# When the row loads of an output projection are requested: two tiles ahead, the last heads in pairs, and the next layer's weights behind them

## The chip, the core and the metric

The kernel runs on one core of one Trainium2 chip. The metric is the device time of one execution in microseconds (us), the median of several. Times inside the kernel come from one profiled execution, read through the hardware profiler's trace. Engines are named as the profile names them: PE (TensorE, matrix multiplication), DVE (VectorE), ACT (ScalarE), POOL (GpSimd) and SP (SyncE, which here does nothing but issue DMAs, so that "SPq" is a queue of DMA issues in program order).

## The reference

A two-layer encoder trunk on x of 1024 rows by 1024 columns, float32. Each layer normalises x, projects it by one matrix, runs three kinds of attention on column slices, gates the results and projects the concatenated heads back:

```python
def hybrid_layer(x, ...):
    h = rms_norm(x, g_norm)
    z = jnp.einsum('bsd,dc->bsc', h, w_in)          # 2656 columns
    ...                                             # A: dense GQA, B: windowed GQA with sink, C: latent attention
    o = jnp.concatenate([oa, ob, oc], axis=-1)      # 1024 rows x 1024 columns
    return x + jnp.einsum('bsm,md->bsd', o, w_out)

for l in range(2):
    h = hybrid_layer(h, ...)
return rms_norm(h, final_g)
```

What the change touches is the last line of a layer, `x + o @ w_out`, and what stands next to it in time: at the end of the first layer the norm of the second layer and the first weights of its input projection, at the end of the second layer the final norm.

## The kernel before

Every float32 product is made from three matmuls: each operand is split into a high part and a low remainder, and h·wh, h·wl and lo·wh are summed. The output projection of a layer works through eight **row tiles** `st` of 128 rows. A tile has two column halves `c` of 512; each half sums over eight heads `m`, with three matmuls for each head, so that one (st, c) has 24 matmuls with 512 columns into a PSUM tile `pw_st_c` (in the names below the layer, `pw0_`, is left out, and a number behind the name is the buffer).

The attention stage has left its result, transposed, in the DRAM tensor `d_o`. The rows of a tile come back in two loads: `ol_st_0` holds heads 0 to 5 (128x6x128, 384 KB, two buffers) and `ol_st_6` heads 6 and 7 (128x2x128, 128 KB, one buffer). ACT casts the high part `oh` from it, and DVE replaces the loaded tile by the remainder (`ol<-ol,oh`). The helper `out_rows` requests a load, `out_hl` requests it if that has not been done and then splits it. `x_row` loads the 512 KB of x (tile `y`) to which the product is added.

The tiles 0 and 1 are mostly computed beside the end of attention; `ab_done` writes their loads. The eight tiles then go through the loop `for st in range(NS)`. In it stand, for each tile: the loads and splits of this tile (`x_row`, `out_hl(0, 6, st)`, `out_hl(6, 8, st)`), its matmuls, the addition to `y`, the store of `y`, the norm of the next layer (`xt`, `rs_x`, DVE scaling with `ng`), its transposition on PE (`pt`), whose results go to the tiles `hTh` and `hTl`.

A scheduler orders the instructions of each engine from the program and its own cost model, so that an instruction can stand on its engine well ahead of or behind its place in the text. Two things limit it. A DMA on SP stands behind the one named in `queue_behind[0]` if that is set (helper `dma`). Buffers limit the rest: a load into a tile with two buffers waits until the matmuls that read the tile two before it are done.

In the loop `queue_behind[0]` names the last load of w_out (`wo_ins[0]`). All DMAs that are written after it are free among themselves, among them the `wst` loads, the weights of the next layer's first projection (`stage.load_wv()` at st == 2, `WV_ST = 2`, and those of the projection behind it). A `wst` load is split by POOL (`wh`) and DVE (`wl`).

The loads of the vectors `ng` (the next norm's scale, spread to 128 rows, 512 KB) and, in the last layer, `fg` stand ahead of the loop.

Of the kernel before, what the change touches and what calls it, by code (L numbers as in the profile page):

```python
# [8 lines left out]
F32 = mybir.dt.float32  # L9
F32R = mybir.dt.float32r  # L10
# [35 lines left out]
def kernel(  # L46
# [22 lines left out]
    P = 128  # L69
    S, D = x.shape[1], x.shape[2]  # L70
    DEPTH = norm_g.shape[0]
    NS = S // P
# [155 lines left out]
    for l in range(DEPTH):  # L228
# [453 lines left out]
        with ExitStack() as ph:  # L682
# [113 lines left out]
            class Gqa:  # L796


                def __init__(self, g, qt, m0):
                    self.g, self.qt, self.m0 = g, qt, m0  # L800
                    self.nm = f"{g}{l}_{qt}"
                    self.q, self.loaded = qstack(g, qt, self.nm)
                    self.sm = small.tile([P, 6], F32, tag=f"sm{g}", name=f"sm{self.nm}")
                    self.o = at.tile([P, 3, P], F32, tag="o", name=f"o{self.nm}", bufs=OBUFS)

                def gate(self):
# [73 lines left out]
            if True:  # L880
# [47 lines left out]
                class UnitB:  # L928
# [7 lines left out]
                    def scores(self):  # L936
                        b, kv, nm, k0, k1 = self.b, self.kv, self.nm, self.k0, self.k1
                        n = self.kts * P
                        mo = (k0 - b.qt + 1) * P
                        mx = small.tile([P, 3], F32, tag="bmx", name=f"bmx{nm}")  # L940
                        scs = at.tile([P, 1152], F32, tag="p", name=f"sc{nm}", bufs=PBUFS)
                        scs = [scs[:, g * 384 : (g + 1) * 384] for g in range(3)]
                        for g in range(3):
                            h = 3 * kv + g
                            ps = ps_s(f"s{nm}_{g}")
                            kr_ = slice(k0 * P, k1 * P)
                            mm3(ps[:, :n], [(b.head(h), ks["b", 0][:, kv, kr_]), (b.head(h), ks["b", 1][:, kv, kr_])])
                            sc = scs[g]
                            V.tensor_tensor_reduce(
                                sc[:, :n],  # L950
                                ps[:, :n],
                                mask[:, mo : mo + n],
                                0.125,
                                -3.0e38,
                                ALU.add,
                                ALU.max,
                                mx[:, g : g + 1],
                            )

                        sk = sink[:, 3 * kv : 3 * kv + 3]  # L960
                        nmb = small.tile([P, 3], F32, tag="bnm", name=f"bnm{nm}")
                        V.tensor_tensor(nmb, mx, sk, ALU.max)
                        V.tensor_scalar(nmb, nmb, -1.0, None, ALU.mult)
                        es = small.tile([P, 3], F32, tag="bes", name=f"bes{nm}")
                        V.tensor_add(es, nmb, sk)
                        A.activation(es, es, AF.Exp)
                        for g in range(3):
                            h = 3 * kv + g
                            A.activation(
                                scs[g][:, :n],  # L970
                                scs[g][:, :n],
                                AF.Exp,
                                bias=nmb[:, g : g + 1],
                                accum_out=b.sm[:, h : h + 1],
                            )
                        smv = b.sm[:, 3 * kv : 3 * kv + 3]
                        V.tensor_add(smv, smv, es)
                        self.scs = scs
# [18 lines left out]
            def ab_done():  # L997
                pk_.close()
                vp_.close()
                wa_.oo = wa_.enter_context(tc.tile_pool(name=f"oo{l}", bufs=1, side="right", reuse_waits="tile"))  # L1000
                wa_.wa = wa_.enter_context(tc.tile_pool(name=f"wa{l}", bufs=1, side="right", reuse_waits="tile"))
                for st in range(2):
                    out_rows(0, 6, st)
                for m in range(MW):
                    load_wo(wa_.wa, m)
                    if m == 0:
                        x_row(0)
                for st in range(2):
                    out_hl(0, 6, st)
                x_row(1)  # L1010
                out_hl(6, 8, 0)

            orows, xrows, wo_ins = {}, {}, {}

            def out_rows(m0, m1, st):

                nm = f"{l}_{st}_{m0}"
                orows[m0, st] = h, lo = [
                    wa_.oo.tile([P, m1 - m0, P], F32R, tag=f"o{t}{m0}", name=f"o{t}{nm}", bufs=1 if m0 else 2)
                    for t in "hl"  # L1020
                ]
                dma(lo, d_o[:, m0:m1, st * P : (st + 1) * P])

            def out_hl(m0, m1, st):
                if (m0, st) not in orows:
                    out_rows(m0, m1, st)
                h, lo = orows[m0, st]
                A.copy(h, lo.bitcast(F32))  # L1028
                V.tensor_sub(lo, lo.bitcast(F32), h.bitcast(F32))  # L1029

            def x_row(st):

# [17 lines left out]
            def out_part(st, c, m0, m1):  # L1050

                if m0 == 0:
                    wa_.ps[st, c] = (ps_o if (2 * st + c) % 4 == 3 else ps_s)(f"pw{l}_{st}_{c}")
                cs = slice(c * 512, (c + 1) * 512)
                for m in range(m0, m1):
                    h, lo = (t[:, m % 6, :] for t in orows[m // 6 * 6, st])
                    wh, wl = (t[:, cs] for t in wa_.w[m])
                    mm3(wa_.ps[st, c], [(h, wh), (h, wl), (lo, wh)], m == 0, m == 7)
                    yield
# [150 lines left out]
        with ExitStack() as ph:  # L1210
# [10 lines left out]
            for st in range(NS):  # L1221
                nm = f"{l}_{st}"
                s_ = slice(st * P, (st + 1) * P)
                if st > 1:
                    x_row(st)
                    out_hl(0, 6, st)
                if st:
                    out_hl(6, 8, st)
                y = xrows[st]
                if last:  # L1230
                    ss = small.tile([P, 2], F32, tag="ss2", name=f"ssf{nm}")
                for c in range(2):
                    cs = slice(c * 512, (c + 1) * 512)
                    for _ in out_part(st, c, MW if (st, c) in wa_.ps else 0, 8):
                        pass
                    ps = wa_.ps[st, c]
                    V.tensor_add(y[:, cs], ps, y[:, cs])
                    if last:
                        jk = wb.tile([P, 512], F32, tag="jk", name=f"jkf{nm}_{c}", bufs=2)
                        A.activation(jk, y[:, cs], AF.Square, accum_out=ss[:, c : c + 1])  # L1240
                        if c == 0:
                            e0 = small.tile([P, 1], F32, tag="e0", name=f"e0{nm}")
                            V.tensor_scalar(e0, ss[:, 0:1], 1.0 / D, EPS, ALU.mult, ALU.add)
                            V.tensor_mul(y[:, cs], y[:, cs], fg[:, cs])
                if last:
                    ms = small.tile([P, 1], F32, tag="ms1", name=f"ms_f{nm}")
                    V.scalar_tensor_tensor(ms, ss[:, 1:2], 1.0 / D, e0, ALU.mult, ALU.add)
                    r = small.tile([P, 1], F32, tag="rs1", name=f"rs_f{nm}")
                    G.tensor_tensor(out=r, in0=ms, in1=mhalf[:, 0:1], op=ALU.pow)
                    tc.keep_in_program_order(nc.vector.tensor_mul(y[:, 512:1024], y[:, 512:1024], fg[:, 512:1024]))  # L1250
                    A.activation(y[:, 0:512], y[:, 0:512], AF.Copy, scale=r[:, 0:1])
                    dma(x_dst[s_, 0:512], y[:, 0:512], nc.scalar)
                    V.tensor_scalar(y[:, 512:1024], y[:, 512:1024], r[:, 0:1], None, ALU.mult)
                    dma(x_dst[s_, 512:1024], y[:, 512:1024])
                    continue
                dma(x_dst[s_, :], y)
                if not last:
                    xt = stage.px.tile([P, D], F32, tag="xt", name=f"xt{l + 1}_{st}", bufs=XTB)
                    stage.norm(st, xt, y, xt)
                    if st == WV_ST:  # L1260
                        stage.load_wv()
                    if st < NS - 1:
                        stage.turn(st, xt, ps_t)
                    else:
                        stage.xt = xt


# [70 lines left out]
```

## Time and profile before

| | |
|---|---|
| median of 3 runs | 1338.37 us (1336.61 to 1343.8) |
| profiled execution | 1340.55 us |
| its span, from first to last instruction | 1338.5 us |
| mean granted TensorE clock | 0.991 of full speed |
| PE busy | 1301.4 us, 97% of the span |
| DVE, ACT, POOL busy | 883.6, 720.3, 530.6 us |
| DMA | 166.46 MB, mean 124 GB/s |

A busy share is a mean over stages that have different limits. The rest of the time of the profiled execution, 1340.55 - 1338.5 = 2.05 us, lies outside the span. Tile numbers in the trace are left out, so `ol<-d_o` stands for all row loads; of one size or one time it can be told which it is from the order of instructions. The profile's line numbers are those of the kernel before: L97 is the DMA helper, L136 the three matmuls, L171 the transposition, L1028 and L1029 the two steps of `out_hl`, L1237 the addition to `y`, L219 the `wl` step of a weight tile.

### The profile page before, as it was taken

The numbers are of one execution on the slowest core, as the hardware profiler recorded it, in microseconds if no ns is written. First come the engines' busy times: TensorE is split into PE (matmuls) and PEld (weight loads), VectorE is DVE, ScalarE is ACT, GpSimd is POOL, SyncE is SP. The second block draws the span as 40 slices with busy tenths as digits, with TensorE's granted clock in tenths as the row PEclk, the third lists the DMA queues.
The fourth block names the chain that finished last, engine by engine and source line by source line (L and its number), as shares of the span: only waits on it lengthen the run. The fifth ranks groups of instructions, "written<-read, shape, count | busy, mean of one in ns | idle before, by whom it ended". The sixth has DMA issues, their size and how long they took to land.

```text
span 1338.5 us, 21710 instructions
## 1 busy us (share of the span) xinstructions
PE 1301.4 (97%) x7320; PEld 1136.0 (85%) x7320; DVE 883.6 (66%) x2242; ACT 720.3 (54%) x1551; POOL 530.6 (40%) x602
## 2 busy tenths in 40 slices
PE   7999999999999999998999999999999999999997
PEld 7888998869898898876898889888799988888786
DVE  6685761068888989855437757600888899888543
ACT  5332341168888988732223324311888888886332
POOL 3520121026766676732014201200367766678110
PEclk8999999999999999998999999999999999999999
DMA  7244559264212521346323344791732225114443
GB/s 252 88 136 136 149 197 266 75 162 115 73 55 62 135 54 52 127 142 204 128 89 105 118 135 151 233 226 58 185 94 60 72 65 146 41 36 145 138 153 114
DMA packets 176878, 166.46 MB, mean 124 GB/s; under 512 B 22528, under 2 KB 149376, under 8 KB 176768
## 3 DMA queue, kind: packets, MB, share of 16 engines
q1 hardware_dynamic: 158016, 140.43, 36.7%
q10 hardware_dynamic: 18752, 24.65, 5.3%
q8 instruction: 58, 0.95, 0.3%
q14 instruction: 52, 0.43, 0.1%
HBM read 107.35 MB, written 57.67 MB: 123 GB/s over the span
## 4 chain that ended last, share of the span: by engine, by line
PE 82%; DMA 6%; DVE 4%; ACT 3%; issue 2%; POOL 2%; SPq 1%; POOLq 0%; DVEq 0%; ACTq 0%
PE pg L136 13%; PE pw L136 12%; PE pzb L114 7%; PE pza L114 7%; PE poa L136 6%; PE sc L136 5%; PE ppa L730 5%; PE pzc L136 4%; PE sa L136 4%; PE ppc L730 4%; PE poc L136 3%; PE pob L136 2%; PE pzv L114 2%; PE pzv L136 2%; PE sb L136 2%
## 5 line engine op out<-in xcount | busy, mean ns | idle before, releaser
L711 DVE CUSTOM_DVE_ANT_0 pa<-sa,zero 128x512 f32<-128x512 f32 x96 | 65.4, 681 | 141.0 <-PE sa L136 136.1
L738 POOL TENSOR_SCALAR ptha<-pfa 128x512 fp32r<-128x512 f32 x96 | 59.5, 620 | 208.0 <-ACT pfa L737 207.8
L739 POOL TENSOR_TENSOR ptla<-pfa,ptha 128x512 fp32r<-128x512 f32 x96 | 124.0, 1292 | 5.7
L136 PE MATMUL sa<-ka,qsta 128*128 128x512 f32 x384 | 124.5, 419 | 1.5 <-DVE nmxc L711 0.8
L136 PE MATMUL sc<-k,qc 128*128 128x512 f32 x384 | 113.5, 411 | 3.2 <-DMA qc<-d_qc 3.2
L721 ACT ACTIVATE pa<-pa,nmxa 128x1024 f32<-128x1024 f32 x96 | 111.4, 1161 | 8.8 <-DVE nmxa L711 8.8
L136 PE MATMUL pw<-woh,oh 128*128 128x512 f32 x256 | 102.6, 407 | 12.0 <-ACT oh L1028 10.1
L730 PE MATMUL ppa<-ident,pa 128*128 128x128 f32 x768 | 106.5, 273 | 0.1
L730 PEld LDWEIGHTS ppa<-ident,pa 128*128 128x128 f32 x768 | 91.5, 141 | 15.3 <-DVE ptla L742 0.6
L136 PE MATMUL pw<-wol,oh 128*128 128x512 f32 x256 | 102.6, 402 | 0.1
L136 PE MATMUL pg<-hTh,wh 128*128 128x512 f32 x256 | 100.5, 393 | 0.0
L136 PE MATMUL pg<-hTh,wl 128*128 128x512 f32 x256 | 100.2, 392 | 0.0
L136 PE MATMUL pg<-hTl,wh 128*128 128x512 f32 x256 | 100.2, 391 | 0.0
L136 PE MATMUL pw<-woh,ol 128*128 128x512 f32 x256 | 99.2, 398 | 0.3 <-DVE ol L1029 0.3
L644 ACT ACTIVATE g<-pg 128x512 f32<-128x512 f32 x32 | 19.1, 598 | 137.6 <-PE pg L136 110.2
L136 PE MATMUL poa<-ptha,vAB 128*128 128x384 f32 x256 | 88.1, 344 | 0.6 <-POOL ptla L739 0.3
L218 POOL TENSOR_SCALAR wh<-wst 128x384 fp32r<-128x384 f32 (+1 forms) x52 | 30.1, 596 | 143.8 <-PE pzb L114 79.2
L136 PE MATMUL poa<-ptla,vAB 128*128 128x384 f32 x256 | 86.6, 338 | 0.0
L721 ACT ACTIVATE pc<-pc,nmxc 128x1024 f32<-128x1024 f32 x64 | 74.0, 1156 | 9.8 <-DVE nmxc L711 9.5
L136 PEld LDWEIGHTS sc<-k,qc 128*128 128x128 f32 x384 | 66.3, 189 | 12.3 <-DVE ob L820 2.6
L711 DVE CUSTOM_DVE_ANT_0 pa<-sa,zero,nmxa 128x512 f32<-128x512 f32 x96 | 71.2, 743 | 3.6 <-PE sa L136 0.7
L136 PEld LDWEIGHTS sa<-ka,qsta 128*128 128x128 f32 x384 | 64.5, 189 | 9.7 <-DVE nmxc L711 2.1
(234 smaller groups left out, 3828.2 us busy)
## 6 DMA issues: line engine op xcount, KB each, us to landing
wst<-in_w_in_dram SPq DMA_DIRECT2D x20, 512.0 KB, 3.7
d_gate<-g ACTq DMA_DIRECT2D x32, 256.0 KB, 2.0
wost<-in_w_out_dram SPq DMA_DIRECT2D x32, 256.0 KB, 2.7
wst<-in_w_in_dram SPq DMA_DIRECT2D x16, 384.0 KB, 4.4
qsta<-d_qa SPq DMA_DIRECT2D x64, 96.0 KB, 2.6
qstb<-d_qb SPq DMA_DIRECT2D x64, 96.0 KB, 2.7
k<-d_kn SPq DMA_DIRECT2D x12, 512.0 KB, 6.7
qc<-d_qc SPq DMA_DIRECT2D x96, 64.0 KB, 2.2
```

Source lines behind the costliest of these rows:

```text
L114: return lambda *a, **k: tc.keep_in_program_order(f(*a, **k))
L136: T.matmul(ps, lhsT=a, rhs=b, start=first and i == 0, stop=last and i == len(parts) - 1)
L218: G.tensor_scalar(h, f, 1.0, 0.0, ALU.mult, ALU.add)
L644: A.activation(g, ps, AF.Silu)
L711: V.tensor_tensor_reduce(p[:, c * 512 : (c + 1) * 512], ps, zero[:, 0:1].to_broadcast([P, 512]), -1.0, nmx[0][:, 0:1] if c else 3.0e38, AL ...
L721: A.activation(p, p, AF.Exp, scale=-1.0, bias=nmx[1][:, 0:1], accum_out=sm)
L730: T.transpose(pt[:, (j - q0) * P : (j - q0 + 1) * P], p[:, j * P : (j + 1) * P], ident)
L738: G.tensor_scalar(hi, f, 1.0, 0.0, ALU.mult, ALU.add)
L739: G.tensor_tensor(out=lo, in0=f, in1=hi.bitcast(F32), op=ALU.subtract)
```

## The change

- At the end of tile `st`'s matmuls the rows 0 to 5 of tile st + 2 are requested and split; before, tile st's own were written at its start.
- Heads 6 and 7 are loaded for two row tiles at once (128x2x256, 256 KB, one buffer), four loads in a layer in place of eight. Each tile's part is split by itself. The first pair is written in `ab_done`.
- After these requests `queue_behind[0]` is set to the last row load, so that SP loads written after it, the `wst` loads among them, stand behind it.
- `x_row(st + 2)` moves to the end of tile st.
- Some tiles of a few columns in the attention stage get fewer buffers (`sm` 3, `bmx`, `bnm`, `bes` 2).

```diff
@@ attention, small tiles
-                    self.sm = small.tile([P, 6], F32, tag=f"sm{g}", name=f"sm{self.nm}")
+                    self.sm = small.tile([P, 6], F32, tag=f"sm{g}", name=f"sm{self.nm}", bufs=3)
...
@@ ab_done
                 x_row(1)
+                out_rows(6, 8, 0, 2)
                 out_hl(6, 8, 0)
...
+            def out_rows(m0, m1, st, n=1):
+                lo = wa_.oo.tile(
+                    [P, m1 - m0, n * P], F32R, tag=f"ol{m0}", name=f"ol{l}_{st}_{m0}", bufs=1 if m0 else 2
+                )
+                wo_ins["o"] = dma(lo, d_o[:, m0:m1, st * P : (st + n) * P])
+                for i in range(n):
+                    orows[m0, st + i] = lo[:, :, i * P : (i + 1) * P]
 
             def out_hl(m0, m1, st):
-                if (m0, st) not in orows:
-                    out_rows(m0, m1, st)
-                h, lo = orows[m0, st]
+                lo = orows[m0, st]
+                h = wa_.oo.tile([P, m1 - m0, P], F32R, tag=f"oh{m0}", name=f"oh{l}_{st}_{m0}", bufs=1 if m0 else 2)
                 A.copy(h, lo.bitcast(F32))
                 V.tensor_sub(lo, lo.bitcast(F32), h.bitcast(F32))
+                for m in range(m0, m1):
+                    orows[m, st] = h[:, m - m0, :], lo[:, m - m0, :]
...
@@ the loop over row tiles
-                if st > 1:
-                    x_row(st)
-                    out_hl(0, 6, st)
-                if st:
-                    out_hl(6, 8, st)
                 y = xrows[st]
...
+                if st < NS - 2:
+                    out_rows(0, 6, st + 2)
+                    out_hl(0, 6, st + 2)
+                    if st % 2:
+                        out_rows(6, 8, st + 1, 2)
+                    queue_behind[0] = wo_ins["o"]
+                if st < NS - 1:
+                    out_hl(6, 8, st + 1)
...
                     else:
                         stage.xt = xt
+                    if st < NS - 2:
+                        x_row(st + 2)
```

How the scheduled programs differ, at the end of the first layer. First SP's queue there, from the norm's scale `ng` on. Before:

```order
L97 DMA ng_7365<-in_norm_g_dram 128x1024
L97 DMA ol_2_0_7494<-d_o_86 128x6x128
L97 DMA ol_1_6_7444<-d_o_86 128x2x128
L97 DMA x_69<-y_0_6818 128x1024
L97 DMA d_o_86<-oc_1_6_7052 128x256
L97 DMA y_2_7491<-in_x_dram 128x1024
L97 DMA wst_1_7564<-in_w_in_dram 128x4x128 x2
L97 DMA wst_2_7573<-in_w_in_dram 128x4x128 x2
L97 DMA wst_3_8284<-in_w_in_dram 128x2x512
L97 DMA wst_4_8292<-in_w_in_dram 128x2x512
L97 DMA ol_3_0_7599<-d_o_86 128x6x128
L97 DMA ol_2_6_7499<-d_o_86 128x2x128
```

The same place of SP's queue with the change:

```order
L97 DMA ng_7365<-in_norm_g_dram 128x1024
L97 DMA ol_2_0_7420<-d_o_86 128x6x128
L97 DMA x_69<-y_0_6816 128x1024
L97 DMA d_o_86<-oc_1_6_7052 128x256
L97 DMA y_2_7451<-in_x_dram 128x1024
L97 DMA ol_3_0_7473<-d_o_86 128x6x128
L97 DMA ol_2_6_7478<-d_o_86 128x2x256
L97 DMA x_69<-y_1_6864 128x1024
L97 DMA ol_4_0_7560<-d_o_86 128x6x128
L97 DMA y_3_7506<-in_x_dram 128x1024
L97 DMA wst_1_7577<-in_w_in_dram 128x4x128 x2
L97 DMA wst_2_7586<-in_w_in_dram 128x4x128 x2
```

Six `wst` loads, `wst_1` to `wst_4`, stood ahead of `ol_3_0`; now none does, and the first comes behind `ol_4_0` and `y_3`. `wst_3` and `wst_4` have moved further back, behind `ol_7_0` and the last pair, `wst_5` and `wst_6` behind `y_7`. `ol_2_0` keeps its place right behind `ng`; `ol_1_6` is gone from here, as it is part of the first pair.

Next PE, the last part of row tile 1, behind the transposition of tile 0 (`pt_0`). Before:

```order
L171 MATMUL pt_0_1_7436<-ident,xt_0_7421 128x128 x4
L136 MATMUL pw_1_0_7318<-woh_7_7389,oh_1_6_7443 128x512
L136 MATMUL pw_1_0_7318<-wol_7_7390,oh_1_6_7443 128x512
L136 MATMUL pw_1_0_7318<-woh_7_7389,ol_1_6_7444 128x512
L136 MATMUL pw_1_1_7334<-woh_5_7369,oh_1_0_6805 128x512
L136 MATMUL pw_1_1_7334<-wol_5_7370,oh_1_0_6805 128x512
L136 MATMUL pw_1_1_7334<-woh_5_7369,ol_1_0_6806 128x512
```

With the change:

```order
L171 MATMUL pt_0_1_7437<-ident,xt_0_7429 128x128 x4
L136 MATMUL pw_1_1_7334<-woh_5_7369,oh_1_0_6861 128x512
L136 MATMUL pw_1_1_7334<-wol_5_7370,oh_1_0_6861 128x512
L136 MATMUL pw_1_1_7334<-woh_5_7369,ol_1_0_6804 128x512
L136 MATMUL pw_1_1_7334<-woh_6_7379,oh_1_6_7425 128x512
L136 MATMUL pw_1_1_7334<-wol_6_7380,oh_1_6_7425 128x512
L136 MATMUL pw_1_1_7334<-woh_6_7379,ol_0_6_6866 128x512
```

The last reader of `ol_1_0`, whose buffer `ol_3_0` takes, has moved four rows forward, from row 2711 of PE's order to row 2707, and the last reader of the first pair (`ol_0_6`) stands on row 2713. The first matmul of tile 3 (`pw_3_0` with `oh_3_0`) stands on row 2731 in both programs, with `oh_2_6` four rows behind it; the transposition of tile 1, `pt_1`, moves from row 2761 to row 2739.

Last DVE, behind the scaling of `xt_1` at which tile 1 ends, with the change:

```order
L164 SCALAR_TENSOR_TENSOR xt_1_7484<-y_1_6864,rs_x_1_7489,ng_7365 128x1024
L1030 TENSOR_TENSOR ol_3_0_7473<-ol_3_0_7473,oh_3_0_7475 128x768
L1030 TENSOR_TENSOR ol_2_6_7478<-ol_2_6_7478,oh_2_6_7480 128x2x128
L178 TENSOR_TENSOR hTl_0_7359<-pt_1_0_7492,hTh_0_7358 128x4x128
L1030 TENSOR_TENSOR ol_4_0_7560<-ol_4_0_7560,oh_4_0_7562 128x768
L178 TENSOR_TENSOR hTl_0_7359<-pt_1_1_7499,hTh_0_7358 128x4x128
L1235 TENSOR_TENSOR y_2_7451<-pw_2_0_7508,y_2_7451 128x512
L219 TENSOR_TENSOR wl_1_7579<-wst_1_7577,wh_1_7578 128x512 x2
L1235 TENSOR_TENSOR y_2_7451<-pw_2_1_7534,y_2_7451 128x512
L1030 TENSOR_TENSOR ol_2_6_7478<-ol_2_6_7478,oh_3_6_7565 128x2x128
L219 TENSOR_TENSOR wl_2_7588<-wst_2_7586,wh_2_7587 128x512 x2
```

Before, the four steps of `wl_1` and `wl_2` stood together right behind the scaling of `xt_0`, ahead of tile 0's `hTl`, and four more (`wl_3`, `wl_4`) around the last addition to `y_1`. Now two stand between the additions to `y_2`, two behind the remainder of `oh_3_6`, and the four others behind the remainders of the last pair.

## Rows read from the trace of the kernel before

**Rows 1.** The page: busy time of each engine, share, instructions.

```profile
PE 1301.4 (97%) x7320; PEld 1136.0 (85%) x7320; DVE 883.6 (66%) x2242; ACT 720.3 (54%) x1551; POOL 530.6 (40%) x602
```

**Rows 2.** Busy time in stretches: length, engines' busy us, PEclk, DMA share, GB/s.

```profile
590.00:600.00 10.00, 7.50 (x32) 5.86 (x31) 3.84 (x6) 2.54 (x5) 2.34 (x2) 0.83 0.24 85
...
630.00:730.00 100.00, 100.00 (x561) 87.19 (x560) 47.72 (x91) 26.73 (x53) 18.20 (x23) 1.00 0.35 110
```

**Rows 3.** PE's waits from 580 to 700: us in total, times, longest.

```profile
PE pw L136 <- ACT oh L1028: 7.8, 2, 5.6
PE pw L136 <- DVE ol L1029: 0.3, 1, 0.3
```

**Rows 4.** The chain that ended last, 585 to 640: start, us, what.

```profile
586.17 6.85 DMA ol<-d_o
593.04 0.84 ACT oh L1028
...
607.82 2.77 DVE wl L219 x3
...
611.06 5.83 DMA ol<-d_o
...
616.97 0.84 ACT oh L1028
...
617.86 9.27 PE pw L136 x30
```

**Rows 5.** The DMA queue of SP in order of time, 585 to 611.

```profile
585.70 0.42 SPq L97 DMA_DIRECT2D ng<-in_norm_g_dram  x1
586.17 4.02 SPq L97 DMA_DIRECT2D ol<-d_o  x2
...
600.29 0.33 SPq L97 DMA_DIRECT2D y<-in_x_dram  x1
600.72 10.24 SPq L97 DMA_DIRECT2D wst<-in_w_in_dram  x6
```

**Rows 6.** Matmuls of `pw` alone, in stretches: PE busy, PEld, DVE, PEclk, DMA.

```profile
611.87:617.86 5.99, 0.40 (x3) 0.01 (x1) 0.68 (x1) 0.82 1.00 280
617.86:622.65 4.79, 4.79 (x11) 3.79 (x12) 0.00 (x0) 0.51 1.04 324
1257.25:1262.00 4.75, 4.75 (x13) 3.43 (x14) 0.68 (x1) 0.64 0.00 0
```

**Rows 7.** The chain that ended last, second layer's projection.

```profile
1249.78 6.56 DMA ol<-d_o
...
1274.27 44.55 PE pw L136 x195
```

**Rows 8.** DMA issues at 632, 611, 628, 585.7 and 600.7: KB, median us to landing.

```profile
ol<-d_o SPq DMA_DIRECT2D x1, 384.0 KB, 3.2
...
ol<-d_o SPq DMA_DIRECT2D x1, 384.0 KB, 5.8
...
ol<-d_o SPq DMA_DIRECT2D x1, 128.0 KB, 2.2
...
ng<-in_norm_g_dram SPq DMA_DIRECT2D x1, 512.0 KB, 6.0
...
wst<-in_w_in_dram SPq DMA_DIRECT2D x4, 256.0 KB, 5.0
```

**Rows 9.** ACT and DVE in order of time, 595 to 599.

```profile
595.50 1.06 ACT L162 ACTIVATE xt<-y 128x1024 f32<-128x1024 f32 x1 [1.62 <-DVE y L1237]
...
597.88 1.28 DVE L164 SCALAR_TENSOR_TENSOR xt<-y,rs_x,ng 128x1024 f32<-128x1024 f32 x1
```

**Rows 10.** ACT at 1226, POOL at 705, in order of time.

```profile
1226.53 0.40 ACT L1028 CAST oh<-ol 128x256 fp32r<-128x256 f32 x1 [2.13 <-DMA ol<-d_o]
...
705.62 1.20 POOL L218 TENSOR_SCALAR wh<-wst 128x512 fp32r<-128x512 f32 x2 [10.62 <-PE pzv L136]
```

More of the change, by code (lines that the diff above doesn't have):

```diff
@@ L939, in scores @@
                         mo = (k0 - b.qt + 1) * P
-                        mx = small.tile([P, 3], F32, tag="bmx", name=f"bmx{nm}")
+                        mx = small.tile([P, 3], F32, tag="bmx", name=f"bmx{nm}", bufs=2)
                         scs = at.tile([P, 1152], F32, tag="p", name=f"sc{nm}", bufs=PBUFS)
@@ L960, in scores @@
                         sk = sink[:, 3 * kv : 3 * kv + 3]
-                        nmb = small.tile([P, 3], F32, tag="bnm", name=f"bnm{nm}")
+                        nmb = small.tile([P, 3], F32, tag="bnm", name=f"bnm{nm}", bufs=2)
                         V.tensor_tensor(nmb, mx, sk, ALU.max)
                         V.tensor_scalar(nmb, nmb, -1.0, None, ALU.mult)
-                        es = small.tile([P, 3], F32, tag="bes", name=f"bes{nm}")
+                        es = small.tile([P, 3], F32, tag="bes", name=f"bes{nm}", bufs=2)
                         V.tensor_add(es, nmb, sk)
@@ L1010, in ab_done @@
                 x_row(1)
+                out_rows(6, 8, 0, 2)
                 out_hl(6, 8, 0)
             orows, xrows, wo_ins = {}, {}, {}
[L1015 to L1022, printed above, removed]
+            def out_rows(m0, m1, st, n=1):
[5 more added lines that the diff above has]
+                    orows[m0, st + i] = lo[:, :, i * P : (i + 1) * P]
             def out_hl(m0, m1, st):
-                if (m0, st) not in orows:
-                    out_rows(m0, m1, st)
-                h, lo = orows[m0, st]
+                lo = orows[m0, st]
+                h = wa_.oo.tile([P, m1 - m0, P], F32R, tag=f"oh{m0}", name=f"oh{l}_{st}_{m0}", bufs=1 if m0 else 2)
                 A.copy(h, lo.bitcast(F32))
                 V.tensor_sub(lo, lo.bitcast(F32), h.bitcast(F32))
+                for m in range(m0, m1):
+                    orows[m, st] = h[:, m - m0, :], lo[:, m - m0, :]
             def x_row(st):
@@ L1055, in out_part @@
                 for m in range(m0, m1):
-                    h, lo = (t[:, m % 6, :] for t in orows[m // 6 * 6, st])
+                    h, lo = orows[m, st]
                     wh, wl = (t[:, cs] for t in wa_.w[m])
@@ L1265 @@
                         stage.xt = xt
+                    if st < NS - 2:
+                        x_row(st + 2)
 _INS = [
```

## The prediction

> **What bounds the kernel now.** I read the page first. PE is busy for 97% of the span [rows 1], so a change pays only where PE stands still or runs below its clock. The busy time in stretches around the output projections shows where that is: between 590 and 600 PE is busy for 7.50 of 10 us, while the 100 us from 630 on are full at a clock of 1.00 [rows 2]. Third, PE's own waits between 580 and 700: only the projection waits, 7.8 us in two pieces for the cast `oh`, the longer one 5.6, and 0.3 for a remainder `ol` [rows 3]. Fourth, the chain that ended last says what is behind the cast [rows 4]. The first piece is `ol_2_0`: its load is issued at 586.17, takes 6.85, is cast by 593.88, and PE goes on at 593.9. The second is `ol_3_0`: issued at 611.06, landed 5.83 later, cast at 616.97, first matmul at 617.86. Ahead of that issue the chain runs through the weight conversions `wl`. SP's queue shows why: behind `y` at 600.29 stand six `wst` issues that take 10.24 us together, because they wait for staging buffers which POOL and DVE free [rows 5]. The row load was ready to go long before; it stood behind weights that nobody needs yet.
>
> The stall costs more than its idle time. The last matmul before it starts at 611.87, 5.99 us before the next [rows 6], where the usual step is 44.55/195 = 0.228 us [rows 7]. So 5.99 - 0.23 = **5.76 us** are idle. The eleven matmuls behind it take 4.79 us at a granted clock of 0.51 [rows 6], which is the lower of the two levels, 1.2 GHz in place of 2.4. At the usual step they take 11 x 0.228 = 2.51, so **2.28 us** more are lost after PE has stood idle. In layer 2 there is one stall, of the first kind: `ol_2_0` issued at 1249.78, 6.56 to landing [rows 7], and from 1257.25 on thirteen matmuls in 4.75 where 2.96 would do [rows 6].
>
> **The change, part by part.** *The weights behind the row loads.* With the change nothing stands on SP between `y_2` (600.29) and `ol_3_0`, so the load goes when its buffer is free. Its buffer is that of `ol_1_0`, whose last reader now stands on PE's row 2707; 23 matmuls lie between its end and row 2731, the first use of `oh_3_0`. That use would come at 611.87 + 0.23 = 612.10 without a wait, so the buffer is free at 612.10 - 23 x 0.228 = 606.9. The load then has the DMA engines nearly to itself. Landing took 3.2 us for this size alone and 5.8 behind weights [rows 8]; I take 3.2, since the weights are now behind it: 610.1. ACT does `xt_1` first: row 2713 ends at 612.10 - 17 x 0.228 = 608.2, the addition to `y` takes at most the 2.77/3 = 0.92 of a `wl` step over as many columns [rows 4], so 609.1, and `xt` 1.06 and a little for its sum [rows 9]: 610.3. The cast takes 0.84 [rows 4]: 611.2, **0.9 us before PE asks**. With 5.8 it is 613.6 and PE waits 1.5.
>
> The pair with heads 6 and 7 is issued when row 2713 is done, 608.2. Its 256 KB lie between 128 KB in 2.2 and 384 KB in 3.2 [rows 8]; midway is 2.7, so 610.9, or 611.4 at 3.2. Cast behind the other one, 0.40 [rows 10], it is ready by 611.8; PE needs it four matmuls after 612.10, at 613.0. `pt_1`, which has moved forward to 613.9 (four matmuls later), needs `xt_1` scaled by DVE: for `xt_0` that was done 597.88 + 1.28 - 595.50 = 3.7 us after ACT's start on it [rows 9], hence 609.1 + 3.7 = 612.8. So the stall goes wholly, with slacks near 1 us: **-5.76 - 2.28 = -8.04**.
>
> *Two heads of tile 1 ahead on PE.* At 593.9 PE now does four matmuls that need only casts before the first remainder, which covers the wait of 0.3 [rows 3]: -0.2.
>
> *The first stalls.* `ol_2_0` keeps its place behind `ng`, in layer 2 behind `fg`. `ng` takes 6.0 us to land and `ol_2_0`, issued 0.47 later [rows 5], takes 6.85 [rows 4], against 3.2 alone [rows 8]. I leave both stalls as they are: 0. The Trainium skill, "DMA: Bandwidth & Descriptors", section "Queues, rings and completion order", has a rule for it: a transfer's completion write on a DMA engine lands only after every earlier write of that engine. By that rule `ol_2_0` cannot be complete before `ng`; the trace agrees (585.70 + 6.0 = 591.7 for `ng`, 593.0 for `ol_2_0`).
>
> *The weights, later.* `wst_1` and `wst_2` are issued behind `ol_4_0` (612.1) and `y_3`, from about 613.1 to 614.3, and land 5.0 later [rows 8], at 619.3; with 8 for the queue ahead of them 622. DVE now converts `wl_1` between the additions to `y_2` and `wl_2` right behind the remainder of `oh_3_6`, which PE needs on row 2788: 613.9 + 0.87 for `pt_1` + 47 x 0.228 = 625.5. From 619.3, POOL's 1.2 [rows 10], two `wl` at 0.92 each, an addition and the remainder make 623.1. Cover is 2.4 us; without it PE waits what is over and loses about 2.3 in clock. Later still: `wst_3` and `wst_4` stand ahead of `y_6`'s addition with some 4 us of room by the order, and the last ones are not urgent, since POOL's `wh` at 705.62 waits 10.62 us for PE, not for data [rows 10]. So 0, at worst +0.5.
>
> *The pairs.* Eight loads become four a layer: four DMA issues fewer on SP, which costs PE nothing either way. The first pair doubles a load at whose end ACT waits: in layer 2 for 2.13 us [rows 10]. 128 KB more at the 280 GB/s of rows 6 are 0.5 us at most; ACT's next exponential moves by that, PE by less. I take +0.1, with bounds 0 and +0.5. The smaller buffers of the attention stage leave all orders there as they were: 0. In layer 2 no weights stand ahead of `ol_3_0`, and its buffer is free four matmuls earlier, while its cast now stands behind a square for the final norm: 0, bounds -0.2 and +0.5.
>
> **The sum.** -8.0 - 0.2 + 0.1 = -8.1 us. The profiled execution would go from 1340.55 to 1332.4. It lies 2.2 above the median of the runs, 1338.37; from the median the same difference gives 1330.3, which I give as **1330.5 us** (-0.6%).
>
> **The rivals.** *The wait comes back in part.* `ol_3_0` lands in 5.8 as before, as `x<-y`, `y` and the pair share the engines: 1.5 of idle plus up to 2.3 at the low clock, so 3.8 of the 8.1 return: 1334.3. For it speaks that 3.2 was seen with the queue quiet; against it, that nothing large is in flight at 606.9.
>
> *No gain.* Another wait on the same path, say `xt_1` or the remainder of `ol_3_0` behind `pt_1` on DVE, stops PE for 5 to 6 us, and the low clock follows again: about 1338. Against it the slacks of 1 us and more, each from a row.
>
> *Slower: the single pair buffer.* A pair can be requested only when the last matmul on the pair before it is done, and PE needs the new one 22 matmuls (5.0 us) later at tile 2, and 28 matmuls and a transposition (7.2 us) later at tiles 4 and 6. Issue, landing, cast and remainder are 0.4 + landing + 0.4 + 0.4, so it decides at a landing above 3.8 and 6.0. At the 6.85 seen behind `ng` the waits are 3.0 and 0.9 us, each with about 2.2 at the low clock: 2 x 5.2 + 4 x 3.1 = 22.8 over both layers, less 8.1: 1353. For it: weights are in flight before tile 4 of layer 1; against it: only 1 MB of them, issued over 10 us before that pair, and none in layer 2. The rule of the Trainium skill named above bears on this too, as a pair's completion would come after that of weights issued ahead of it; no row of the kernel before shows a pair behind weights.
>
> *Better.* Without `ol_1_6` beside it `ol_2_0` lands as if alone, and both first stalls go, about 4 us each with their slow matmuls: 1322. Against it `ng`, which is still ahead; half of that, 1326, is the nearest I would give weight to.
>
> **Chances.** The stall goes and nothing returns: 0.68. In part 0.15, no gain 0.08, slower 0.05, better 0.04. The range reaches from the better half-case to past the partial return: 1327.0 to 1336.5; what lies outside is most of the last three. A difference of 0.5% is 6.7 us, about what a measurement of this kernel can tell from no change, and that line is at 1331.7, so close to the forecast that a fifth of the main case falls short of it. Faster: 0.68 x 0.8 + 0.04 = 0.58; slower 0.05; within 0.5% the rest, 0.37.
>
> **What would show it.** In the changed profile PE's waits between 580 and 700 hold one wait of 2.2 for `oh` and none of 5.6; the stretch from 600 to 630 is full at clock 1.00; `ol_3_0` is issued near 606.9 and lands within 3.5; `wst` issues start after 612. A first stall at 593.9 that is shorter, a wait of PE for `oh` at tiles 4 or 6, or an `ol` landing above 6 there would make it wrong, as would a new wait for `wl` through `y_2`.

## The result, and the profile after

The changed kernel takes 1328.21 us (median of 6 runs, 1326.7 to 1331.22), the kernel before in its runs beside it 1337.76: the ratio is 0.9928, interval [0.9911, 0.9946]. The difference of 9.5 us, 7.2 to 11.9 by the interval, is a little more than the 8.1 forecast. The profiled execution took 1331.22 us with a span of 1329.4, against 1340.55 and 1338.5.

PE's waits of the changed kernel from 580 to 700, which answer to [rows 3]:

```profile
PE pw L136 <- ACT oh L1029: 2.0, 1, 2.0
```

The wait of 5.6 us and that for a remainder are gone; one of 2.0 is left. The chain that ended last, in the same stretch as [rows 4] (start, us, what):

```profile
586.34 6.58 DMA ol<-d_o
592.92 0.02 issue
592.94 0.84 ACT oh L1029
593.78 0.04 issue
593.83 11.00 PE pw L136 x40
604.82 0.87 PE pt L171 x8
605.70 7.76 PE pw L136 x34
613.46 0.87 PE pt L171 x8
614.33 13.89 PE pw L136 x61
```

The first half reads as before: `ol_2_0` behind the vector, 6.6 us. From 593.83 on the chain holds nothing but PE, where before it went through `wl`, a DMA and a cast. Busy time in stretches (length, PE, PEld, DVE, ACT, POOL, PEclk, DMA share, GB/s):

```profile
590.00:600.00 10.00, 7.97 (x36) 6.46 (x35) 4.26 (x6) 2.55 (x5) 1.30 (x2) 0.83 0.29 102
600.00:610.00 10.00, 10.00 (x50) 8.34 (x49) 2.83 (x5) 2.41 (x5) 0.03 (x1) 1.00 0.38 103
610.00:620.00 10.00, 10.00 (x50) 8.33 (x49) 5.44 (x7) 3.37 (x6) 0.79 (x2) 1.00 0.84 264
```

From 610 to 620 fifty matmuls run at a clock of 1.00; before, PE was idle for over half of this and the clock behind it was 0.51 [rows 6]. SP's queue, in order of time, shows why:

```profile
599.28 0.33 SPq L97 DMA_DIRECT2D y<-in_x_dram  x1
606.43 1.75 SPq L97 DMA_DIRECT2D ol<-d_o  x2
608.54 0.33 SPq L97 DMA_DIRECT2D x<-y  x1
611.67 0.36 SPq L97 DMA_DIRECT2D ol<-d_o  x1
612.61 0.34 SPq L97 DMA_DIRECT2D y<-in_x_dram  x1
613.00 2.42 SPq L97 DMA_DIRECT2D wst<-in_w_in_dram  x4
```

`ol_3_0` is issued at 606.43, forecast 606.9, in place of 611.06, and the weights follow at 613.0, forecast 613.1. The DMA issues from 606 to 608 (KB, us to landing), then ACT and PE in order of time:

```profile
ol<-d_o SPq DMA_DIRECT2D x1, 384.0 KB, 3.3
ol<-d_o SPq DMA_DIRECT2D x1, 256.0 KB, 3.4
```

```profile
609.81 0.83 ACT L1029 CAST oh<-ol 128x768 fp32r<-128x768 f32 x1
611.32 0.41 ACT L1029 CAST oh<-ol 128x256 fp32r<-128x256 f32 x1 [0.67 <-DMA ol<-d_o]
```

```profile
611.93 0.39 PE L136 MATMUL pw<-woh,oh 128*128 128x512 f32 x1
...
612.84 0.39 PE L136 MATMUL pw<-woh,oh 128*128 128x512 f32 x1
```

The row load lands in 3.3 us (I took 3.2), its cast ends at 610.64, 1.3 us ahead of PE's first use at 611.93. The pair takes 3.4, not the 2.7 I took, and its cast ends at 611.73, 1.1 us ahead of PE's use at 612.84.

How long each projection takes can be read from one kind of its matmuls (ns min/median/max, first and last start). Before, first and second layer:

```profile
L136 PE MATMUL pw<-woh,oh x128: 387/389/796, 563.8 to 682.2; 128*128 128x512 f32 x128
L136 PE MATMUL pw<-woh,oh x128: 387/389/658, 1226.8 to 1330.9; 128*128 128x512 f32 x128
```

With the change:

```profile
L136 PE MATMUL pw<-woh,oh x128: 387/389/628, 563.9 to 673.5; 128*128 128x512 f32 x128
L136 PE MATMUL pw<-woh,oh x128: 387/389/628, 1218.1 to 1321.8; 128*128 128x512 f32 x128
```

The first layer's projection goes from 118.4 to 109.6 us, the second's from 104.1 to 103.7. These 8.8 and 0.4 us are the whole 9.1 by which the span is shorter, to rounding: nothing was gained elsewhere.

### The profile page after: what moved, and what is told of

Same layout as the page of the kernel before. It is cut to its first block, busy times and chain, and to the rows that moved or that the text cites. A ratio compares the mean times of both kernels' runs of the same rounds, so it can differ in the third digit from the quotient of the medians.

```text
span 1329.4 us, 21686 instructions
## 1 busy us (share of the span) xinstructions
PE 1298.0 (98%) x7320; PEld 1134.1 (85%) x7320; DVE 883.2 (66%) x2242; ACT 720.8 (54%) x1551; POOL 530.3 (40%) x602
## 4 chain that ended last, share of the span: by engine, by line
PE 83%; DMA 5%; POOL 3%; ACT 3%; DVE 2%; issue 2%; SPq 1%; POOLq 0%; ACTq 0%; DVEq 0%
PE pg L136 13%; PE pw L136 11%; PE poa L136 7%; PE pzb L114 7%; PE pza L114 7%; PE ppa L730 5%; PE pzc L136 5%; PE sa L136 5%; PE sc L136 4%; PE ppc L730 3%; PE poc L136 3%; PE pob L136 2%; PE sb L136 2%; PE pzv L114 2%; PE pzv L136 2%
## 5 line engine op out<-in xcount | busy, mean ns | idle before, releaser
L730 PE MATMUL ppc<-ident,pc 128*128 128x128 f32 x512 | 71.9, 273 | 0.8 <-ACT rbb L792 0.7
```

The lines of the kernel that those rows point to most:

```text
L730: T.transpose(pt[:, (j - q0) * P : (j - q0 + 1) * P], p[:, j * P : (j + 1) * P], ident)
```

## The experiments

All times are medians in us. The kernel before was run beside the kernels of each of three groups (e1 to e4, e5 to e8, e9 to e11); between groups the ratios are to be compared.

| run | kernel | time | before | ratio, interval |
|---|---|---|---|---|
| e1 | changed, weights free on the queue | 1338.02 | 1338.28 | 1.0001 [0.9988, 1.0013] |
| e2 | before, weights behind row loads | 1326.48 | 1338.28 | 0.9916 [0.9903, 0.993] |
| e3 | changed, no pairs | 1330.08 | 1338.28 | 0.9942 [0.993, 0.9955] |
| e4 | changed, vector behind `ol_2_0` | 1323.85 | 1338.28 | 0.9897 [0.9883, 0.9912] |
| e5 | changed, again | 1329.2 | 1339.81 | 0.9915 [0.9902, 0.9927] |
| e6 | as e3, again | 1332.67 | 1339.81 | 0.9944 [0.9931, 0.9956] |
| e7 | changed, no early requests | 1334.62 | 1339.81 | 0.9955 [0.9943, 0.9966] |
| e8 | changed, vector loaded by ACT | 1324.56 | 1339.81 | 0.9883 [0.987, 0.9896] |
| e9 | as e4, again | 1323.31 | 1340.15 | 0.9886 [0.9869, 0.9903] |
| e10 | as e4, no pairs | 1325.25 | 1340.15 | 0.9896 [0.9879, 0.9914] |
| e11 | changed, 512 KB more ahead of `ol_2_0` | 1334.27 | 1340.15 | 0.9961 [0.9948, 0.9975] |

### e1: the weights free again

```diff
-                    queue_behind[0] = wo_ins["o"]
```

> The changed kernel without its last line on the queue: the weight loads are again free to stand ahead of the row loads, and by the program's order they do (wst_1 to wst_4 ahead of ol_3_0, as before); early requests and pairs stay. Theory (the place of ol_3_0 behind the weights on SP is the whole stall): PE waits 5 to 6 us for oh near 612 again, the landing of ol_3_0 is 5 us or more, and the time goes back to 0.998 to 1.001 of the kernel before, 1336 to 1339 us. Rival (the early request and the pairs bring the gain, the queue does not matter): 0.992 to 0.994, 1327 to 1330 us, no wait near 612.

The whole gain is gone. SP's queue and PE's first matmul of tile 3 in this kernel, in order of time:

```profile
599.72 10.06 SPq L97 DMA_DIRECT2D wst<-in_w_in_dram  x6
609.88 1.00 SPq L97 DMA_DIRECT2D ol<-d_o  x2
...
616.09 0.79 PE L136 MATMUL pw<-woh,oh 128*128 128x512 f32 x1 [6.00 <-ACT oh L1029]
616.68 0.63 PE L136 MATMUL pw<-wol,oh 128*128 128x512 f32 x1
617.11 0.63 PE L136 MATMUL pw<-woh,oh 128*128 128x512 f32 x1
```

These are the rows of before: six weight issues of 10 us, the row load behind them, a wait of 6.0, and matmuls that start 0.43 apart in place of 0.23. Early requests and pairs alone bring nothing that can be told from zero (the interval reaches 1.7 us to either side), since the program order of a request does not set its place on the queue. The theory holds, the rival falls.

### e2: the order alone

```diff
@@ the kernel before
-                dma(lo, d_o[:, m0:m1, st * P : (st + 1) * P])
+                wo_ins["o"] = dma(lo, d_o[:, m0:m1, st * P : (st + 1) * P])
...
                 if st:
                     out_hl(6, 8, st)
+                    queue_behind[0] = wo_ins["o"]
```

> The kernel before with one thing alone: DMAs written after a tile's row loads stand behind them on SP. Requests stay at their own tile, heads 6 and 7 are loaded tile by tile. By the program's order only wst_1 and wst_2 (1 MB) still stand ahead of ol_3_0, wst_3 to wst_6 have gone behind the last row loads. Theory: ol_3_0 is issued when its buffer is free, near 607, but lands behind 1 MB of weights in 5 to 6 us, so PE waits 0.5 to 2.5 us near 612 and then runs slow for about 2 us: 1331 to 1334 us, ratio 0.995 to 0.998. Rival (the order alone is enough): 1328 to 1330 us, no wait. Rival (only the early request helps): 1336 us or more, wait of 5 us.

It is faster than I expected, and as fast as the changed kernel as far as the intervals tell (ratio 0.9916 against 0.9928, and 0.9915 in e5): one line of order, without early requests and pairs, brings as much. The first rival was right as to the wait near 612. PE's waits from 580 to 700, then ACT in order of time:

```profile
PE pw L136 <- ACT oh L1028: 0.9, 1, 0.9
```

```profile
594.32 0.40 ACT L1028 CAST oh<-ol 128x256 fp32r<-128x256 f32 x1 [0.46 <-DMA ol<-d_o]
594.63 0.36 ACT L763 COPY ohc<-poc 64x256 f32<-64x256 f32 x1
596.63 0.84 ACT L1028 CAST oh<-ol 128x768 fp32r<-128x768 f32 x1 [1.64 <-DMA ol<-d_o]
```

`ol_3_0` is issued at 606.68 and lands behind 1 MB of weights in 5.5, as expected, but PE does not wait for it. By the program's order the scheduler has also put the rest of row tile 1 ahead of tile 2 on PE, so that tile 1's buffers come free sooner and tile 3 is asked for 14 rows later (twelve matmuls and the transposition of tile 1). For the same reason the first wait is not for `ol_2_0`, whose cast ends at 597.5 without a wait of PE, but 0.9 us for the small load of heads 6 and 7. The edit is one line, but it is not one effect: the order of PE changed with it.

### e3, e6 and e10: without the pairs

```diff
@@ ab_done
-                out_rows(6, 8, 0, 2)
+                out_rows(6, 8, 0)
@@ the loop
-                    if st % 2:
-                        out_rows(6, 8, st + 1, 2)
-                    queue_behind[0] = wo_ins["o"]
                 if st < NS - 1:
+                    out_rows(6, 8, st + 1)
+                    queue_behind[0] = wo_ins["o"]
                     out_hl(6, 8, st + 1)
```

> The changed kernel with heads 6 and 7 loaded tile by tile as before (eight loads of 128 KB a layer); early requests and order stay. Theory (pairs cost and bring nearly nothing): 1328 to 1330 us, ratio 0.993 to 0.995, PE's only waits in the projections those at the first use of oh of tile 2, with 0.3 us for a remainder in layer 1 of the trunk since PE's order ahead of it is again that of before. Rival (the pairs bring the part of the gain beyond 8.1): 1 us or more slower than the changed kernel. Rival (the pairs cost, by the load at the end of which ACT waits): faster than the changed kernel by 0.5 us or more.

The kernel is 1.9 us slower than the changed one was in its own runs, but the two intervals overlap. So I ran both beside each other (e5, e6):

> The changed kernel itself once more, as the measure for the runs beside it on the same chip. By both theories 1326.5 to 1331 us, ratio 0.992 to 0.994; if runs differ by the low clock behind the first waits, a run with a granted clock of 0.993 is 2 to 4 us longer than one of 0.997.

> The changed kernel with heads 6 and 7 loaded tile by tile, now beside the changed kernel. In e3 it was 1330.1 against 1328.2 us measured apart. Theory (pairs bring little): within 1 us of the changed kernel beside it. Rival (pairs bring what exceeds the 8.1 forecast): 1.5 to 2.5 us slower than it.

Now the difference is 3.5 us, and the intervals of the two ratios do not touch: the kernel with pairs is the faster one, where I had the pairs at +0.1. PE's waits of e6 from 580 to 700:

```profile
PE pw L136 <- ACT oh L1029: 1.7, 1, 1.7
PE pw L136 <- DVE ol L1030: 0.3, 1, 0.3
```

The 0.3 us for a remainder, which the pairs had covered by two casts that stand ready, are back, but the wait ahead of it is 0.3 us shorter: both kernels wait 2.0 us in this projection. The waits do not explain the difference. e10 is to take the first wait away as well (the edit of e4 added to the above):

> The kernel of e4 with heads 6 and 7 loaded tile by tile. With pairs the changed kernel was 1.9 and 3.5 us faster than without (e3, e6). Theory (the pairs act only through the first wait: two casts of two tiles stand ready for PE before the first remainder, so that the 0.3 us wait and part of the slow matmuls go): with the first wait gone the pairs are worth nothing, within 1 us of e9. Rival (the pairs save on the DMA queue throughout): 2 us or more slower than e9.

It is 1.9 us slower than e9 beside it, but the intervals overlap widely, so this does not decide between the two. Nor is the first wait quite gone in the first layer, as the theory asks, where e9 has no wait for `oh` or `ol`:

```profile
PE pw L136 <- ACT oh L1029: 0.3, 1, 0.3
PE pw L136 <- DVE ol L1030: 0.3, 1, 0.3
```

### e4 and e9: the vector behind the first row load

```diff
             if last:
                 fg = wb.tile([P, D], F32, name="fg", bufs=1)
-                dma(fg, final_g.partition_broadcast(P))
-            else:
-                dma(stage.ng, norm_g[l + 1].partition_broadcast(P))
+            out_rows(0, 6, 2)
+            queue_behind[0] = wo_ins["o"]
+            if last:
+                dma(fg, final_g.partition_broadcast(P))
+            else:
+                dma(stage.ng, norm_g[l + 1].partition_broadcast(P))
...
-                    out_rows(0, 6, st + 2)
+                    if st:
+                        out_rows(0, 6, st + 2)
```

> The changed kernel with the 512 KB loads of ng and fg moved on SP's queue from right ahead of ol_2_0 to right behind it. Theory (ol_2_0 lands late because the vector's load is ahead of it): ol_2_0 lands in 3.3 to 4.5 us in place of 6.3 to 6.6, both first waits of PE (2.0 us each) and the slow matmuls behind them (1.7 us each) go: 7.5 us off the changed kernel, 1320 to 1322 us, ratio 0.987. Rival (the two loads share the DMA engines whichever is first): landing 5.5 us or more, half of the wait stays, 1325 to 1328 us. Rival (what the vector feeds becomes late: the scaling of xt_0 or of y_0): no gain, and DVE waits for ng.

PE's order is the same as in the changed kernel, row for row. Neither projection has a wait for `oh` any more. The DMA issues from 585.5 to 588 (KB, us to landing):

```profile
ng<-in_norm_g_dram SPq DMA_DIRECT2D x1, 512.0 KB, 5.6
ol<-d_o SPq DMA_DIRECT2D x1, 384.0 KB, 4.9
```

`ol_2_0` takes 4.9 us in place of 6.6: late enough to tell that the vector behind it still takes part of the DMA engines, early enough for PE. The gain is 4.4 us on the median, less than the 7.5 expected. The 7.5 counted on the low clock behind both first waits, as in the first profile of the changed kernel: e4's profiled execution (1323.56) is 7.7 us shorter than that one (1331.22), but 3.2 shorter than e5's (1326.75), which has the low clock behind neither. Again:

> The kernel of e4 once more (vectors behind ol_2_0, pairs), as the measure for e10 and e11 beside it. 1322.5 to 1325.5 us, ratio 0.988 to 0.991, no wait of PE for oh in either projection.

1323.31 us, with an interval that ends at 0.9903 (0.9912 in e4), where those of the changed kernel begin at 0.9911 and, in e5, 0.9902. This version beats the kernel before by far more than the uncertainty, and the changed kernel by 4 to 6 us, at the edge of what the intervals separate.

### e8: the vector loaded during attention

```diff
-                dma(fg, final_g.partition_broadcast(P))
+                dma(fg, final_g.partition_broadcast(P), nc.scalar)
...
-                dma(stage.ng, norm_g[l + 1].partition_broadcast(P))
+                dma(stage.ng, norm_g[l + 1].partition_broadcast(P), nc.scalar)
```

> The changed kernel with the loads of ng and fg issued by ACT during attention, long before ol_2_0. Theory (ol_2_0 is late by what is ahead of it on the DMA engines): it lands in 3.2 to 3.5 us, the first waits of PE are gone, 1322 to 1325 us as in e4. Rival (the wait belongs to the late issue of ol_2_0, behind the store of attention's result on SP, not to the vector): the landing is as short but a wait of 0.5 us or more stays, 1326 us or more. Against both: ACT's own work is delayed by the issue, under 0.5 us a layer.

The DMA issue of `ol_2_0` at 589.6 (KB, us to landing):

```profile
ol<-d_o SPq DMA_DIRECT2D x1, 384.0 KB, 3.4
```

With nothing of the vector beside it the load lands in 3.4, and PE has no wait for `oh` in either projection, though the load is issued 3.3 us later than in the changed kernel. But PE's order has changed here too: six matmuls of tile 1 now stand ahead of tile 2. PE begins them at 592.97 and `oh_2_0` at 594.34, and the cast ends at 593.92, so that by the changed kernel's order a wait of about 1.0 us would be left (an estimate from these rows). The absence of a wait in e8 therefore does not refute the rival that blames the late issue; e4 does, where PE's order is unchanged, the load is issued no earlier (586.71 against 586.34) and the wait is gone. Nor is the time of this run the landing's alone.

### e11: more ahead of the first row load

```diff
+            more = dram.tile([P, D], F32, name=f"more{l}")
+            dma(more, x_src[0:P, :])
             for st in range(NS):
```

> The changed kernel with one more transfer of 512 KB (a copy of 128 rows of x within DRAM, whose result nothing reads) ahead of ol_2_0 in each layer, behind the vector. Theory (what stands ahead of ol_2_0 sets its landing, and PE pays its wait and the slow matmuls behind it): landing 1.5 to 4 us longer, 8 to 10.5, the two waits of PE 3.5 to 6 us each, slow matmuls worth 1.7 to 2.3 us behind each in every run: 1332 to 1340 us, ratio 0.995 to 1.001. Rival (the landing is set by ol_2_0 itself or its late issue): unchanged, 1327 to 1330 us.

SP's queue in order of time, the DMA issues from 588 to 592 (KB, us to landing), and PE's waits from 580 to 700:

```profile
588.94 0.42 SPq L97 DMA_DIRECT2D ng<-in_norm_g_dram  x1
589.41 0.56 SPq L97 DMA_DIRECT2D more<-in_x_dram  x1
590.01 0.58 SPq L97 DMA_DIRECT2D ol<-d_o  x1
```

```profile
ng<-in_norm_g_dram SPq DMA_DIRECT2D x1, 512.0 KB, 6.2
more<-in_x_dram SPq DMA_DIRECT2D x1, 512.0 KB, 6.9
ol<-d_o SPq DMA_DIRECT2D x1, 384.0 KB, 7.6
```

```profile
PE pw L136 <- ACT oh L1029: 3.6, 1, 3.6
```

The landing goes up by 1.0 us, less than the 1.5 to 4 of the theory, and the wait by 1.6, as the load is also issued 0.6 us further behind `ng` (1.07 against 0.47). In the second layer the landing is 6.6 and the wait 3.3, where the changed kernel has 6.3 and 2.0, and in e5 5.4 and 1.1. The time rises by 4 to 6 us by ratio (0.9961 against the changed kernel's 0.9928 and, in e5, 0.9915). In the first layer the landing goes from 3.4 with nothing over 4.9 with the vector behind and 6.6 with the vector ahead to 7.6 with a further 512 KB: it follows what shares the engines, and most what stands ahead. The last step is the least certain, as one program's landing can differ by 0.9 us between two executions (6.3 and 5.4 above), and a few rows of PE's order have moved in e11.

### e7: without the early requests

```diff
@@ the loop: requests at the start of their own tile
+                if st > 1:
+                    x_row(st)
+                    out_rows(0, 6, st)
+                    out_hl(0, 6, st)
+                    if st % 2 == 0:
+                        out_rows(6, 8, st, 2)
+                if st:
+                    out_hl(6, 8, st)
+                    queue_behind[0] = wo_ins["o"]
                 y = xrows[st]
...
-                if st < NS - 2:
-                    out_rows(0, 6, st + 2)
-                    out_hl(0, 6, st + 2)
-                    if st % 2:
-                        out_rows(6, 8, st + 1, 2)
-                    queue_behind[0] = wo_ins["o"]
-                if st < NS - 1:
-                    out_hl(6, 8, st + 1)
...
-                    if st < NS - 2:
-                        x_row(st + 2)
```

> The changed kernel without the early requests: row loads are written at the start of their own tile as before, pairs and the order behind the row loads stay. wst_1 and wst_2 stand ahead of ol_3_0 again, and PE asks for oh_3_0 14 rows and a transposition later than in the changed kernel and for oh_4_0 right after. Theory from e2 (the order on the queue brings the gain, the early request nothing): no wait above 1 us behind 600, 1326 to 1330 us. Rival (the early request keeps the loads of tiles 3 and 4 off PE's path): a wait of 1 to 3 us for oh near 612 to 618 and slow matmuls behind it, 1331 us or more.

The rival was right. PE in order of time, and the DMA issues from 610 to 613:

```profile
617.35 0.58 PE L136 MATMUL pw<-woh,oh 128*128 128x512 f32 x1 [3.33 <-ACT oh L1029]
```

```profile
ol<-d_o SPq DMA_DIRECT2D x2, 384.0 KB, 6.0
```

`ol_3_0` and `ol_4_0` are issued behind 1 MB of weights and take 6.0 us each; PE waits 3.3 us. Beside e5 the kernel is 5.4 us slower, though still 5.2 faster than the kernel before. So in the kernel with pairs the early request is not idle: the weights are held only behind requests that are written before them, and with requests two tiles ahead `ol_3_0` and `ol_4_0` are among these. In e2 the same `wst` loads stood ahead of `ol_3_0`, but the queue ran 4 us earlier there: `ol_2_6`, which is ahead of the weights and waits for a buffer of tile 1, was issued at 602.79 in e2 and at 606.59 in e7, and `ol_3_0` at 606.68 and 610.67. With single loads and its own order on PE, e2 needs no early request.

## Why the prediction was right, and where a size was off

**The stall at tile 3.** Right in place, cause and size. Forecast were 5.76 us of idle and 2.28 of slow matmuls; PE's wait of 5.6 has gone and the stretch behind it runs at 1.00. e1 shows the cause: with the weights free on the queue the wait is 6.0 again and the time is that of before; and in e2 the order alone, with the other order on PE that comes with it, takes the wait away. The steps on the way (606.9, 3.2, 611.2, 613.1, 623.1) came out as 606.43, 3.3, 610.64, 613.00 and 623.44, the last one being the end of the remainder of `oh_3_6` on DVE, to be read off this row with its neighbour `wl_2` behind it:

```profile
623.03 0.41 DVE L1030 TENSOR_TENSOR ol<-ol,oh 128x256 fp32r<-128x256 f32 x1
623.36 1.28 DVE L219 TENSOR_TENSOR wl<-wst,wh 128x512 fp32r<-128x512 f32 x2
```

Two of these steps hide errors that did no harm. The terms named for 623.1 come to as much as 623.7, if the addition takes the 0.92 allowed for one elsewhere and the remainder 0.4. And the four weight loads landed in 6.2 us (median), not 5.0.

**The wait for a remainder.** In the first layer it is gone, as forecast. In the second one of 0.3 us has come in its place, which I had not seen.

**The first stalls.** Forecast 0; in the first profile each is 0.2 us shorter (2.02 and 1.98 against 2.23 and 2.24). The prediction named a shorter first stall as a sign against it, but in e5, the same program, the two waits are 2.0 and 1.1, so that 0.2 us tell nothing. That what stands ahead of `ol_2_0` sets its landing is borne out by e4, e8 and e11. The Trainium skill, "DMA: Bandwidth & Descriptors", section "Queues, rings and completion order", lets a completion land only after earlier writes of the same DMA engine. The order of landings in e11 agrees (595.1, 596.3, 597.6, each issue plus its time), but e4 shows that this is not all of it: with the vector behind, 1.5 us of the extra 3.2 stay (4.9 against 3.4).

**The pairs.** Forecast +0.1, with bounds 0 and +0.5. The cost that it named is not steady: ACT's wait at the end of the first pair in layer 2 rose from 2.13 [rows 10] to 2.62, but over all profiles it lies between 1.95 and 3.00 with pairs (eight of them) and between 2.13 and 2.33 without (five). Against the forecast, the kernel without pairs is 1.9, 3.5 and 1.9 us slower in three comparisons (e3, e6, e10), the middle one alone clear of its intervals. What the pairs would gain is not shown. PE's waits for `oh` and `ol` in both projections make 3.4 us in e5 and 3.6 in e6. The projections, read as in the section on the result, take 108.0 and 101.3 us in e5, 108.1 and 101.9 in e3, and 109.9 and 101.5 in e6, where the low clock (0.83 from 590 to 600, 1.00 in e5) lengthens the first; e10's are 1.1 and 0.0 us longer than e9's, while its whole profiled execution is 4.8 us longer. And in e1 pairs and early requests gave nothing. So that the pairs belong in the sum with -2 or more is not shown, and the cause of the three differences stays open.

**The sum.** -8.1 was forecast, and in the profiled executions the span fell by 9.1 us, 8.8 of them in the projection where the stall was: right in place and nearly in size. That the medians differ by 9.5, and by 10.6 in e5 (9.8 to 13.1 by its interval), has a likely reason in the term for the first stalls. Its 0 keeps the low clock behind them in every execution. The profiled execution of the changed kernel, the slowest of its six, has it behind both, at a mean granted clock of 0.993; the five others have 0.996 or 0.997, a mean that among the profiles goes with at most one fall of the clock after the kernel's first 30 us (e3, e4, e5, e9, e10). That is an argument, not a trace: runs that were not profiled do not show where their clock fell.

**The rivals.** The wait came back in no part; the single pair buffer held nothing up in the first layer: the pair at tile 2 landed in 3.4 us, below the 3.8 from which it decides there, those at tiles 4 and 6 in 4.3 and 4.5, below 6.0. The better case, both first stalls gone, needs the vector moved (e4), and gives 4 to 6 us (e4, e9) where I had priced 8.

## What to carry to other kernels

When a load is late, look at what the issues ahead of it on its queue were waiting for: requesting it earlier in the program did nothing as long as the scheduler could put other transfers ahead (e1), and with pairs an explicit order left a wait of 3.3 us for a request written late (e7). The explicit order alone, one line in the kernel before, gained as much as the whole change (e2), so try the smallest edit by itself. A one-line edit to an order moves rows on every engine, so compare the order of the engine that waits before crediting a difference to the edit (e2 and e8 against e4). After a stall is removed, read the next wait in the same way: the 512 KB vector ahead of the first row load was worth 4 to 6 us more.

## What the runs showed of the hardware that was not expected

The low clock follows a wait of PE in some executions and not in others. The changed kernel's profiled execution and that of e5 are the same program with the same first wait of 2.0 us. Matmuls of the first projection in each (ns min/median/max, first and last start):

```profile
L136 PE MATMUL pw<-woh,oh x128: 387/389/628, 563.9 to 673.5; 128*128 128x512 f32 x128
```

```profile
L136 PE MATMUL pw<-woh,oh x128: 387/389/509, 564.4 to 672.4; 128*128 128x512 f32 x128
```

In the first the longest matmul is 628 ns and the projection takes 109.6 us, in the second 509 ns and 108.0. The stretches tell it by the clock, 0.83 against 1.00 from 590 to 600. In e11 a wait of 3.6 us in layer 1 was followed by the low clock and one of 3.3 in layer 2 was not, while 5.6 us before and 6.0 in e1 were. Each time it comes it costs 1.7 to 2.3 us here, which is part of the spread of 4.5 us over the changed kernel's runs, and why I would no longer count it as certain behind a wait of 2 us. It also comes where the change does nothing: from 300 to 305 us, in the first layer's attention, e2, e3, e5 and e8 have a mean clock of 0.66 and the changed kernel's first profile has 1.00, so that a difference of 2 us between two medians need not come from the edit.
